# One transformer layer on one core: the residual's sum on VectorE in half rows, a new order of the input's first steps, HGRN output one step later, hints on two branches

## The chip, the cores and the metric

The kernel runs on one core of a Trainium2 chip. TensorE (PE in the rows, PEld for its weight loads) multiplies, VectorE (DVE) and ScalarE (ACT) work element by element, GpSimd (POOL) does so too, and SyncE (SP) issues the transfers from device memory. Each engine takes its instructions in order; "PEq", "SPq" and so on in a row are the queue side of an engine. The metric is the time of one execution in microseconds on the device.

## The reference, cut to what matters

256 tokens of 1024 features, one layer, float32 throughout.

```
x = layer_norm(x, ln_in_g, ln_in_b)
h = x @ w_in + b_in                      # 14 blocks of 512 columns and 8 forget gates
fox_o = fox_attention(fq, fk, fv, log_sigmoid(ff))           # 8 heads
o = hgrn2_chunkwise(silu(hq), (1 - lb) * sigmoid(-hf), hi, logf)   # 8 heads
o = rms_norm(o) * hgrn_norm_g * silu(hg)
mixed = (sigmoid(g0) * (fox_o @ w_fox) + sigmoid(g1) * (o @ w_hgrn)) @ w_mix_out + b_mix_out
x = layer_norm(ALPHA * x + mixed, ln1_g, ln1_b)
x = layer_norm(ALPHA * x + moe(x), ln2_g, ln2_b)   # 16 experts, top 2 of the top group
```

## The kernel before, in words

**The front** (to about 250 us) is everything up to the router. The weights of the mixer come as 15 "front tiles" of 2 MB through a ring of three slots (`load_front`, line 84). Each front tile is cut into 8 units of 512 columns. Every product is made in three passes of exact halves: `prep(u)` (lines 159 to 166) casts a unit to `hi` on ScalarE (line 164; three units on VectorE, line 162) and subtracts to get `lo` on VectorE or on GpSimd (line 165, chosen by `on_pool(u)`), and `mm(u)` multiplies (lines 185 to 187 for "tm" tiles, 198 to 200 for "fm" tiles). The main loop runs over steps `i = 2 .. 59`; a step is two units, 2i and 2i+1, and in it come, in this order: `pe[i]`, `prep(2i+3)`, `mm(2i)`, the evacuation of finished products, `post[i]`, `prep(2i+4)`, `mid[i]`, `mm(2i+1)`. The tables `pe`, `mid` and `post` are filled by `at(table, step, function)` and so set by hand the order on PE, ACT, DVE and POOL. SyncE's order is left to the scheduler. A ring slot is free for the next front tile when the last unit of the old one has been prepared.

**What the change touches.** `x_turn`, `x_affine`, `x_hi`, `x_lo` bring the normalised input to features on partitions as halves (lines 225 to 250); they and the first four units stand before the loop. `resid` (lines 316 to 322) turns `xraw`, the normalised input, into `ALPHA * (x * g + b) + b_mix`, for the sum ahead of the first norm at step 53 and later (`mix_add`). `small` makes the lower bounds `lbt` of the forget gates. `h_exps(j)`, `h_mul(j)`, `h_scores(j)`, `h_mask(h)`, `h_out(h)` are the HGRN heads, two heads for each j: decays, scaled queries and keys (DVE, ACT), scores (PE), masked copies `hst` (DVE, ACT), and the sums of values (PE, lines 577 to 579). `h_check` loads a flag on four engines (line 593) and branches on it (line 594): over code for extreme decays, which these inputs do not take. A second such branch (line 1484) stands near the end, over code for experts' lists that are too long.

**The experts** (from about 250 us) take their weights, 201 MB, through some eleven slots of 2 MB. A slot's next load is issued where the instructions that read the old weights stand (`load_exp`, `load_parts`: lines 864 and 891), and waits on SyncE's queue until they are done. The front's ring becomes three of these slots. The first expert's weights are loaded during the front.

Of the kernel before, what the change touches and what calls it, by code (L numbers as in the profile page):

```python
# [23 lines left out]
# the last two experts: the down projection's weights come by columns, a half and two quarters  # L24
LAST = NE - 2

# columns of the constant pack
# [8 lines left out]
# columns of the row pack  # L36
# [10 lines left out]
def trunk(ctx: ExitStack, tc: tile.TileContext, x, cst_d, rows_d, wf, we, lvl_d, out):  # L47
# [24 lines left out]
    def bank(tag, shape, name=None):  # L72
        """one bank; g: products and all that comes and goes, s: scores, o: sums kept for long"""
        return ps.tile(shape, F32, name=name or tag, tag=tag, bufs={"g": 4, "s": 2, "o": 2}[tag])

    # ---- loads, in the order of use
# [57 lines left out]
    def stats(tt, c, src, n=256):  # L134
        """pieces of a row, of equal widths"""
        V.bn_stats(sm[:, 24 * tt + 6 * c:24 * tt + 6 * c + 6], src)

    def ln_scale(tt, n):
        """(mean, 1/sqrt(var + eps))"""
        mv = mvs(tt)  # L140
        V.bn_aggr(mv, sm[:, 24 * tt:24 * tt + 6 * n])
        A.activation(mv[:, 1:2], mv[:, 1:2], AF.Sqrt, bias=eps_in[:, 0:1])
        V.reciprocal(mv[:, 1:2], mv[:, 1:2])
        return mv

    # ---- products in three passes of exact halves; a unit: 512 columns of a weight tile
# [4 lines left out]
    def on_pool(u):  # L151
        return u in (0, 1, 2) or 24 <= u < 56 and u % 2 == 1 or u >= 56 and u % 4 == 3
# [19 lines left out]
    def mm(u, tts=(0, 1)):  # L172
# [3 lines left out]
        if KIND[i] == "tm":  # L176
            for tt in tts:
                if c == 0:
                    # the very last sums in two banks, so that their ends can overlap
# [24 lines left out]
    # ---- input norm  # L204
    def halves(name):
        """exact halves of eight blocks of features, in four parts"""
# [16 lines left out]
    def x_turn(tt, j):  # L223
        """two blocks of features, a bank each pair"""
# [28 lines left out]
    def x_parts(tt, j):  # L253
# [13 lines left out]
    warm(2, 128)  # L267
    prep(0)
    prep(1)
    x_affine(0, 0)  # L270
    x_affine(0, 1)
    x_stats(1)
    x_hi(0, 0)
    x_hi(0, 1)
    x_lo(0, 0)
    mm(0, (0,))
    V.bn_aggr(mvs(1), sm[:, 24:36])
    x_lo(0, 1)
    mm(1, (0,))
    prep(2)  # L280
    A.activation(mvs(1)[:, 1:2], mvs(1)[:, 1:2], AF.Sqrt, bias=eps_in[:, 0:1])
# [33 lines left out]
    # residual with the output bias: alpha * (x * g + b) + b_mix  # L315
    gA, bA, bM = inr
    resid = [lambda: (G.tensor_scalar(bA, bA, ALPHA, 0.0, op0=OP.mult, op1=OP.add),
                      G.tensor_scalar(gA, gA, ALPHA, 0.0, op0=OP.mult, op1=OP.add)),
             lambda: G.tensor_add(bA, bA, bM)]
    for tt in range(2):  # L320
        resid.append(lambda tt=tt: G.tensor_mul(xraw[:, tt, :], xraw[:, tt, :], gA))
        resid.append(lambda tt=tt: G.tensor_add(xraw[:, tt, :], xraw[:, tt, :], bA))

    # lower bounds of the forget gates: cumsum(softmax) - its first row, over one layer
# [7 lines left out]
    def small():  # L332
        V.tensor_tensor(e0, C("lb"), C("lb"), op=OP.subtract)
        # exp(x) as sigmoid(x) / sigmoid(-x)
        A.activation(e1, e0, AF.Sigmoid, scale=-1.0)
        A.activation(e0, e0, AF.Sigmoid)
        V.reciprocal(e1, e1)
# [5 lines left out]
        V.tensor_scalar(nbhf, C("bhf"), -1.0, None, op0=OP.mult)  # L343
# [14 lines left out]
    # tensors of the mixer  # L358
# [48 lines left out]
    # ---- HGRN2  # L407
# [7 lines left out]
    def hgrn_general(oh):  # L415
        """the same scores for any decays: pairs of tokens by the highest bit in which they differ;
        every exponent is at most zero"""
# [3 lines left out]
        for j in range(4):  # L421
# [38 lines left out]
            # between chunks: from the end of the key's chunk to the start of the query's  # L460
# [43 lines left out]
    def h_exps(j):  # L504
# [7 lines left out]
        # half of the chunk's decay as the reference point: exponents of both signs, at most  # L512
        # half the decay; beyond SAFE the general path below recomputes the scores
# [6 lines left out]
        # between chunks: from the key's reference point to the query's  # L520
# [18 lines left out]
    # two heads side by side: each on its half of the tensor engine's rows  # L539
# [21 lines left out]
    def transposed(p, val, sts, j):  # L561
        """two heads' sums of values: features on partitions, the scores' keys there too"""
# [28 lines left out]

    def h_check():
        big = nc.values_load(hfl, engines=(ET.PE, ET.Activation, ET.DVE, ET.Pool), min_val=0, max_val=1)
        with tc.If(big > 0):  # L594
# [19 lines left out]
    def feat_pe(ot):  # L614
        """[tokens, 512] to features on partitions"""
# [10 lines left out]
    # ---- forgetting attention  # L626
# [6 lines left out]
    def f_proj():  # L633
        """the eight blocks of features on four groups of columns"""
# [17 lines left out]
    def f_log():  # L652
        """log forget gates, tokens on partitions"""
# [3 lines left out]
        # log_sigmoid(f) = min(f, 0) + log(sigmoid(|f|))  # L657
# [11 lines left out]
    def f_sum(j):  # L669
        """cumulative gates of the keys, on every partition: columns as the scores'"""  # L670
# [28 lines left out]
    def f_soft(h):  # L699
        """negated logits; F[t] is the same along a row and cancels under the row's maximum"""  # L700
# [39 lines left out]
    # ---- merge gates, branches, output projection  # L740
# [53 lines left out]
    # router's weights with the norm's scale, each column centred: (r - mean) @ w = r @ centred w  # L794
# [32 lines left out]
    # ---- stream of the experts' weights: in the order of use, two experts at a time  # L827
# [10 lines left out]
    def load_exp(pl, n=1):  # L838
        for _ in range(n):
# [5 lines left out]
            if nxt[0] >= len(order) - 4:  # L845
                # in pairs, a part of each by turns
# [20 lines left out]
    # slots of four parts, the first that are used, so that loads go on as early as can be. One tile lies apart:  # L867
    # half of it comes before, with the first tile's second half, the rest in that one's place
# [3 lines left out]
    def slot(pl):  # L872
        """a slot's parts"""
# [20 lines left out]
    def claim(pl):  # L894
        """the next tile's place, its parts to be loaded one by one"""
# [717 lines left out]
```

## Time and profile before

| what | us |
|---|---|
| three runs | 703.16, 705.47, 705.56 |
| their median | 705.47 |
| span of the profiled execution (first to last instruction) | 704.5 |
| PE busy in it | 661.4 (94%) |
| mean granted clock of PE | 0.974 |
| DVE, ACT, POOL busy | 210.1, 188.5, 93.1 |
| moved by transfers | 238.75 MB, mean 339 GB/s |

The profiled execution's own time is not listed apart from its span; the span lies 1.0 us under the median of the runs and inside their range. Matmuls are pipelined, so a busy PE in a row is not PE at its peak. [...]

### The profile page before, as it was taken

The page shows a single profiled execution, that of the slowest core. Times are in us where ns is not written, and L with a number is a line of the kernel's source. Part 1 is how long each engine was busy: PE and PEld are TensorE (multiplying, and loading weights), DVE is VectorE, ACT ScalarE, POOL GpSimd, SP SyncE. Part 2 cuts the span into 40 slices and gives each one's busy share as a digit, 9 for nine tenths or more (in the row PEclk, how much of TensorE's full clock was granted, in tenths as well). Part 3 has the DMA queues.
Part 4 walks back from the last instruction along what each step waited for, and adds up shares of the span by engine and source line. Part 5 has one row for each costly group of instructions (what it writes and reads, how often), then busy time and mean ns, then how long its engine had stood idle before and what let it go on. Part 6 is the DMA issues. An engine that isn't in the chain of part 4 may idle for free.

```text
span 704.5 us, 9357 instructions
## 1 busy us (share of the span) xinstructions
PE 661.4 (94%) x3707; PEld 388.1 (55%) x3707; DVE 210.1 (30%) x457; ACT 188.5 (27%) x389; POOL 93.1 (13%) x83
## 2 busy tenths in 40 slices
PE   6779998999999999999999999999999999699986
PEld 5678797899998953534534443443443433243433
DVE  5776862654468521100100100100100100100015
ACT  4536354577645421102012010010010010010211
POOL 2632344433136000000000000000000000000001
PEclk8979999999999999999999999999999999999999
DMA  8926633543978969999999999999999999999981
GB/s 330 382 105 225 270 121 123 194 178 118 360 287 300 397 206 375 425 394 429 425 407 424 421 412 421 424 412 421 420 417 419 418 420 416 418 425 410 412 331 60
DMA packets 40520, 238.75 MB, mean 339 GB/s; under 512 B 4496, under 2 KB 4624, under 8 KB 32400
## 3 DMA queue, kind: packets, MB, share of 16 engines
q1 hardware_dynamic: 40464, 238.02, 84.3%
q8 instruction: 33, 0.54, 0.3%
q14 instruction: 23, 0.19, 0.1%
HBM read 236.95 MB, written 1.05 MB: 338 GB/s over the span
## 4 chain that ended last, share of the span: by engine, by line
PE 67%; DMA 13%; DVE 2%; ACT 0%; issue 0%; DVEq 0%; SPq 0%; ACTq 0%
PE g L1276 25%; DMA w<-in_we_dram 13%; PE g L1293 13%; PE g L1248 3%; PE g L198 3%; PE g L199 3%; PE g L200 3%; PE acc L1301 3%; PE g L186 1%; PE g L187 1%; PE g L185 1%; PE g L1312 1%; PE g L1422 1%; PE g L1284 1%; PE g L1116 1%; DVE e L1465 1%
## 5 line engine op out<-in xcount | busy, mean ns | idle before, releaser
L1276 PE MATMUL g<-w,e 128*64 128x512 f32 x992 | 219.7, 595 | 2.4 <-DMA w<-in_we_dram 2.4
L1276 PEld LDWEIGHTS g<-w,e 128*64 128x64 f32 x992 | 69.0, 137 | 138.6 <-issue 125.8
L1293 PE MATMUL g<-w,f 128*64 128x512 f32 x448 | 106.5, 604 | 2.4 <-DMA w<-in_we_dram 2.4
L165 DVE TENSOR_TENSOR lo<-w,hi 128x512 fp32r<-128x512 f32 x85 | 69.1, 824 | 62.1 <-ACT hi L164 61.3
L164 ACT CAST hi<-w 128x512 fp32r<-128x512 f32 x117 | 70.4, 620 | 54.2 <-PE g L199 39.3
L198 PE MATMUL g<-xp,hi 128*128 128x256 f32 x256 | 76.3, 298 | 9.0 <-DVE hv L374 9.0
L199 PE MATMUL g<-xp,hi 128*128 128x256 f32 x256 | 74.2, 290 | 0.0
L200 PE MATMUL g<-xp,lo 128*128 128x256 f32 x256 | 74.0, 289 | 0.0
L1293 PEld LDWEIGHTS g<-w,f 128*64 128x64 f32 x448 | 39.2, 138 | 59.5 <-issue 54.5
L1523 POOL TENSOR_TENSOR e<-e,par 128x256 f32<-128x256 f32 x2 | 1.4, 726 | 459.4 <-DVE nmr L1519 459.4
L165 POOL TENSOR_TENSOR lo<-w,hi 128x512 fp32r<-128x512 f32 x35 | 47.4, 1357 | 109.6 <-ACT hi L164 109.6
L198 PEld LDWEIGHTS g<-xp,hi 128*128 128x128 f32 x256 | 50.8, 199 | 11.3 <-issue 10.4
L199 PEld LDWEIGHTS g<-xp,hi 128*128 128x128 f32 x256 | 50.9, 199 | 0.1
L200 PEld LDWEIGHTS g<-xp,lo 128*128 128x128 f32 x256 | 50.8, 199 | 0.0
L1479 DVE COPY f<-g 128x512 f32<-128x512 f32 x7 | 4.8, 692 | 115.2 <-PE g L1293 115.2
L1248 PEld LDWEIGHTS g<-e,raw 128*128 128x128 f32 x224 | 26.1, 191 | 19.8 <-DVE e L1240 10.0
L1248 PE MATMUL g<-e,raw 128*128 128x128 f32 x224 | 28.7, 281 | 8.1 <-DVE e L1240 8.1
L1259 ACT ACTIVATE e<-g,cst 128x128 f32<-128x128 f32 x28 | 10.6, 457 | 68.7 <-PE g L1248 68.7
L1463 DVE TENSOR_TENSOR e<-e,g 128x512 f32<-128x512 f32 x8 | 5.5, 688 | 73.5 <-ACT e L1462 73.5
L185 PE MATMUL g<-hi,xp 128*128 128x512 f32 x48 | 20.7, 431 | 6.5 <-PEq L594 3.4
L1471 ACT COPY f<-g 128x512 f32<-128x512 f32 x8 | 4.7, 586 | 79.9 <-PE g L1284 79.9
L1301 PE MATMUL acc<-f,e 128*128 128x512 f32 x56 | 25.9, 605 | 0.0
(318 smaller groups left out, 745.5 us busy)
## 6 DMA issues: line engine op xcount, KB each, us to landing
w<-in_we_dram SPq DMA_DIRECT2D x49, 2048.0 KB, 17.7
w<-in_we_dram SPq DMA_DIRECT2D x178, 512.0 KB, 10.4
w<-in_wf_dram SPq DMA_DIRECT2D x13, 2048.0 KB, 8.4
w<-in_wf_dram SPq DMA_DIRECT2D x8, 512.0 KB, 9.1
w<-in_we_dram SPq DMA_DIRECT2D x16, 256.0 KB, 6.0
rbc<-in_rows_dram SPq DMA_DIRECT2D x1, 1036.0 KB, 15.9
f<-in_we_dram SPq DMA_DIRECT2D x4, 256.0 KB, 7.6
out_dram<-par SPq DMA_DIRECT2D x4, 256.0 KB, 2.1
```

The lines of the kernel that those rows point to most:

```text
L164: A.copy(hi, src)
L165: (G if on_pool(u) else V).tensor_sub(lo, src, hi.bitcast(F32))
L185: PE.matmul(p, rh(c)[:, t], hi[:, a:b], start=c == 0, stop=False, skip_group_check=True)
L186: PE.matmul(p, rh(c)[:, t], lo[:, a:b], start=False, stop=False, skip_group_check=True)
L198: PE.matmul(p, hi[:, w], rh(k), start=k == 0, stop=False)
L199: PE.matmul(p, hi[:, w], rl(k), start=False, stop=False)
L200: PE.matmul(p, lo[:, w], rh(k), start=False, stop=k == nk - 1)
L1248: PE.matmul(p[:, i, :], raw[:, tt, k * 128:(k + 1) * 128], oneh2[:, tt, :], start=tt == 0, stop=tt == 1)
L1259: A.activation(t[:, i, :], p[:, i, :], AF.Identity, bias=C("b1")[:, 4 + i:5 + i], scale=C("g1")[:, 4 + i:5 + i])
L1276: PE.matmul(h[64 * nh:64 * nh + 64, :], xg[kh][:, k, 64 * (e % 2):64 * (e % 2) + 64], wcol(e, m + kh, k, nh), start=kh + k == 0, stop=kh = ...
L1293: PE.matmul(py[nh][64 * a:64 * a + 64, :], hT[a][:, c0:c0 + 64], wt[:, nh * 512:nh * 512 + 512], start=f == 0, stop=f == 7)
L1301: PE.matmul(acc[tt][nh], GT[:, tt, :], y[nh], start=start, stop=False, skip_group_check=True)
```

## The change

It does six things. (1) The residual's sum moves from seven GpSimd instructions on 1024 columns at steps 4 to 9 to ten VectorE instructions on 512 columns, one at each of the steps 5 to 14, with ALPHA folded in. (2) Units 0 and 1 get their `lo` on VectorE, no more on GpSimd. (3) The first four steps of the input (`x_affine` to `x_lo` for its first two pairs of blocks) stand ahead of `prep(0)`, and six warming products stand in the place of two. (4) `small` is cut in two: its first part stands at step 2, the rest (`small1`) at step 3. (5) `h_out` stands one step later. (6) Each of the two branches gets a hint, "LikelyTaken", on four engines.

```diff
-        return u in (0, 1, 2) or 24 <= u < 56 and u % 2 == 1 or u >= 56 and u % 4 == 3
+        return u == 2 or 24 <= u < 56 and u % 2 == 1 or u >= 56 and u % 4 == 3
...
-    warm(2, 128)
+    warm(6, 128)
+    x_affine(0, 0)
+    x_affine(0, 1)
+    x_hi(0, 0)
+    x_lo(0, 0)
+    x_hi(0, 1)
+    x_lo(0, 1)
     prep(0)
     prep(1)
-    x_affine(0, 0)
-    x_affine(0, 1)
+    mm(0, (0,))
     x_stats(1)
-    x_hi(0, 0)
-    x_hi(0, 1)
-    x_lo(0, 0)
-    mm(0, (0,))
     V.bn_aggr(mvs(1), sm[:, 24:36])
-    x_lo(0, 1)
     mm(1, (0,))
+    A.activation(mvs(1)[:, 1:2], mvs(1)[:, 1:2], AF.Sqrt, bias=eps_in[:, 0:1])
     prep(2)
-    A.activation(mvs(1)[:, 1:2], mvs(1)[:, 1:2], AF.Sqrt, bias=eps_in[:, 0:1])
...
-    resid = [lambda: (G.tensor_scalar(bA, bA, ALPHA, 0.0, op0=OP.mult, op1=OP.add),
-                      G.tensor_scalar(gA, gA, ALPHA, 0.0, op0=OP.mult, op1=OP.add)),
-             lambda: G.tensor_add(bA, bA, bM)]
+    resid = []
+    for h in range(2):
+        resid.append(lambda c=slice(512 * h, 512 * h + 512): V.scalar_tensor_tensor(
+            bA[:, c], bA[:, c], ALPHA, bM[:, c], op0=OP.mult, op1=OP.add))
     for tt in range(2):
-        resid.append(lambda tt=tt: G.tensor_mul(xraw[:, tt, :], xraw[:, tt, :], gA))
-        resid.append(lambda tt=tt: G.tensor_add(xraw[:, tt, :], xraw[:, tt, :], bA))
+        for h in range(2):
+            c = slice(512 * h, 512 * h + 512)
+            resid.append(lambda tt=tt, c=c: V.scalar_tensor_tensor(
+                xraw[:, tt, c], xraw[:, tt, c], ALPHA, gA[:, c], op0=OP.mult, op1=OP.mult))
+            resid.append(lambda tt=tt, c=c: V.tensor_add(xraw[:, tt, c], xraw[:, tt, c], bA[:, c]))
...
+    def h_hint():
+        tc.mark_branch_hint_location("hgrn", "LikelyTaken", engines=ENG4)
...
-        with tc.If(big > 0):
+        with tc.If(big > 0, label="hgrn"):
...
-    at(post, 3, small)
+    at(post, 2, small)
+    at(post, 3, small1)
...
-        at(post, 4 + n, r)
+        at(post, 5 + n, r)
...
-            at(pe, 17 + 2 * j, h_out, h)
+            at(pe, 18 + 2 * j, h_out, h)
...
+    at(post, 23, h_hint)
...
+        if e == LAST:
+            tc.mark_branch_hint_location("slots", "LikelyTaken", engines=ENG4)
```

In the built program both hints stand at the very start of each of the four engines, not where they are marked; the one for the second branch ("slots") stands ahead of the one for the first ("hgrn"). On SyncE, three of the first expert's loads and one of 2 MB move ahead of the load of front tile 6, which they stood behind or around.

On VectorE, steps 2 to 5 of the loop: `lbt` are the bounds that `small` makes, `lo` the lower halves of units 7 to 11, `hv` the first front tile's finished products, taken out of PSUM. Before:

```order
L165 TENSOR_TENSOR lo<-w,hi 128x512 x4
L333 TENSOR_TENSOR lbt<-cst 128x4
L337 RECIPROCAL lbt<-lbt 128x4
L338 TENSOR_TENSOR lbt<-lbt 128x4
L339 RECIPROCAL lbt<-lbt 128x4
L340 TENSOR_TENSOR lbt<-lbt 128x4
L341 TENSOR_TENSOR lbt<-lbt 128x4
L342 TENSOR_SCALAR lbt<-lbt 128x4
L343 TENSOR_SCALAR lbt<-cst 128x4
L165 TENSOR_TENSOR lo<-w,hi 128x512 x2
L374 TENSOR_TENSOR hv<-g,rbc 128x512 x2
L165 TENSOR_TENSOR lo<-w,hi 128x512 x2
```

and in the changed kernel:

```order
L166 TENSOR_TENSOR lo<-w,hi 128x512 x2
L338 TENSOR_TENSOR lbt<-cst 128x4
L342 TENSOR_SCALAR lbt<-cst 128x4
L166 TENSOR_TENSOR lo<-w,hi 128x512 x2
L345 RECIPROCAL lbt<-lbt 128x4
L346 TENSOR_TENSOR lbt<-lbt 128x4
L347 RECIPROCAL lbt<-lbt 128x4
L348 TENSOR_TENSOR lbt<-lbt 128x4
L349 TENSOR_TENSOR lbt<-lbt 128x4
L350 TENSOR_SCALAR lbt<-lbt 128x4
L166 TENSOR_TENSOR lo<-w,hi 128x512 x2
L381 TENSOR_TENSOR hv<-g,rbc 128x512 x2
```

The same instructions stand ahead of `hv`, two of the small ones now ahead of two `lo`.

On VectorE, steps 12 and 13: `ff` and `lfr` are the forget gates of the attention, which wait for a logarithm on ScalarE, `B` to `Dd` the first decays of the HGRN heads. Before:

```order
L384 SCALAR_TENSOR_TENSOR hqt<-g,cst,hqt 128x256
L664 TENSOR_SCALAR ff<-ff 128x16
L665 TENSOR_TENSOR ff<-ff 128x16
L666 CAST lfr<-ff 128x16
L667 TENSOR_TENSOR lfr<-ff,lfr 128x16
L162 CAST hi<-w 128x512
L165 TENSOR_TENSOR lo<-w,hi 128x512
L510 SCALAR_TENSOR_TENSOR B<-rst,lf 128x256
L515 TENSOR_SCALAR hrg<-B 128x4
```

and in the changed kernel:

```order
L391 SCALAR_TENSOR_TENSOR hqt<-g,cst,hqt 128x256
L327 TENSOR_TENSOR raw<-raw,in_inb 128x512
L674 TENSOR_SCALAR ff<-ff 128x16
L675 TENSOR_TENSOR ff<-ff 128x16
L676 CAST lfr<-ff 128x16
L677 TENSOR_TENSOR lfr<-ff,lfr 128x16
L163 CAST hi<-w 128x512
L166 TENSOR_TENSOR lo<-w,hi 128x512
L325 SCALAR_TENSOR_TENSOR raw<-raw,in_ing 128x512
L517 SCALAR_TENSOR_TENSOR B<-rst,lf 128x256
L522 TENSOR_SCALAR hrg<-B 128x4
```

One instruction of the residual is new ahead of `ff`, and one ahead of `B`; a third stands ahead of the products of step 14.

On PE, HGRN output of heads 0 and 1 (`o<-hv,hst`) stood alone between two units of products, step 17:

```order
L200 MATMUL g<-xp,lo 128x256
L577 MATMUL o<-hv,hst_116 128x64
L578 MATMUL o<-hv,hst_116 128x64
L579 MATMUL o<-hv,hst_116 128x64
L577 MATMUL o<-hv,hst_117 128x64
L578 MATMUL o<-hv,hst_117 128x64
L579 MATMUL o<-hv,hst_117 128x64
L198 MATMUL g<-xp,hi 128x256
```

and in the changed kernel, step 18:

```order
L584 MATMUL o<-hv,hst_116 128x64
L585 MATMUL o<-hv,hst_116 128x64
L586 MATMUL o<-hv,hst_116 128x64
L584 MATMUL o<-hv,hst_117 128x64
L585 MATMUL o<-hv,hst_117 128x64
L586 MATMUL o<-hv,hst_117 128x64
L555 MATMUL s<-qp,kp 128x128 x2
L557 MATMUL s<-qx,kp 64x64 x2
L555 MATMUL s<-qp,kp 128x128 x2
L557 MATMUL s<-qx,kp 64x64 x2
L560 MATMUL s<-qx,kx 128x128 x2
```

It stands right ahead of the next pair's scores, two units of products later.

## Rows read from the trace of the kernel before

**Rows 1.** The page: GB/s moved, in 40 equal slices of 17.6 us.

```profile
GB/s 330 382 105 225 270 121 123 194 178 118 360 287 300 397 206 375 425 394 429 425 407 424 421 412 421 424 412 421 420 417 419 418 420 416 418 425 410 412 331 60
```

**Rows 2.** Stretches: busy us and instructions of each engine, clock, DMA share, GB/s.

```profile
core 0: us, PE busy (x) PEld busy (x) DVE busy (x) ACT busy (x) POOL busy (x), PEclk, DMA share, GB/s
...
31.40:40.40 9.00, 0.01 (x2) 0.03 (x1) 8.93 (x8) 0.90 (x3) 8.84 (x5) 0.76 0.32 136
40.40:46.00 5.60, 5.59 (x27) 5.60 (x27) 3.91 (x6) 0.93 (x2) 1.47 (x1) 0.50 0.00 0
46.00:63.50 17.50, 17.50 (x147) 17.50 (x146) 11.50 (x25) 10.60 (x22) 1.29 (x1) 0.99 0.53 189
82.20:87.20 5.00, 5.00 (x29) 5.00 (x30) 4.90 (x15) 1.70 (x5) 1.58 (x1) 0.66 1.03 428
121.30:124.70 3.40, 3.40 (x10) 2.62 (x9) 1.29 (x2) 1.21 (x3) 1.28 (x1) 0.51 0.00 0
...
260.00:680.00 420.00, 404.75 (x1918) 164.86 (x1914) 41.89 (x70) 46.78 (x98) 0.00 (x0) 1.00 1.01 414
```

**Rows 3.** SyncE's waits, 225 to 262 us: total, times, longest.

```profile
SPq L891 <- PE g L1422: 13.7, 6, 9.3
```

**Rows 4.** The chain that ended last, 575 us to the end: start, us, what.

```profile
589.55 10.18 DMA w<-in_we_dram
...
676.35 4.47 DMA w<-in_we_dram
...
680.95 3.52 PE g L1312 x16
```

**Rows 5.** PE's waits, 0 to 250 us: total, times, longest.

```profile
PE g L198 <- DVE hv L374: 9.0, 1, 9.0
PE g L185 <- PEq L594: 3.4, 1, 3.4
PE o L577 <- DVE hst L558: 1.5, 1, 1.5
```

**Rows 6.** Timeline of POOL, 24 to 66 us: last of the residual's seven.

```profile
39.19 2.69 POOL L322 TENSOR_TENSOR raw<-raw,in_inb 128x1024 f32<-128x1024 f32 x1
```

**Rows 7.** Timeline of DVE, 24 to 66 us.

```profile
29.48 2.12 DVE L340 TENSOR_TENSOR lbt<-lbt 128x4 f32<-128x4 f32 x1
31.63 2.26 DVE L341 TENSOR_TENSOR lbt<-lbt 128x4 f32<-128x4 f32 x1
33.93 0.17 DVE L342 TENSOR_SCALAR lbt<-lbt 128x4 f32<-128x4 f32 x1
...
36.23 3.43 DVE L165 TENSOR_TENSOR lo<-w,hi 128x512 fp32r<-128x512 f32 x2
39.58 1.27 DVE L374 TENSOR_TENSOR hv<-g,rbc 128x512 f32<-128x512 f32 x2
```

**Rows 8.** Groups of DVE by line and form, 46 to 64 us.

```profile
L165 DVE TENSOR_TENSOR lo<-w,hi 128x512 fp32r<-128x512 f32 x11 | 7.6, 692 | 6.2 <-ACT hi L164 6.0
```

**Rows 9.** Timeline near the end.

```profile
699.63 0.73 DVE L1534 SCALAR_TENSOR_TENSOR par<-par,sm,g 128x512 f32<-128x512 f32 x1
```

**Rows 10.** Line 594, the first branch on PE: least, middle and most ns, start.

```profile
L594 PEldq COMPARE_BRANCH  x1: 5280/5280/5280, 114.8 to 114.8; - x1
```

**Rows 11.** Timeline, the first 50 us, all engines.

```profile
9.01 1.14 ACT L164 CAST hi<-w 128x512 fp32r<-128x512 f32 x2 [3.49 <-DMA w<-in_wf_dram]
9.71 3.92 POOL L165 TENSOR_TENSOR lo<-w,hi 128x512 fp32r<-128x512 f32 x3 [8.56 <-ACT hi L164]
...
11.20 0.50 PE L185 MATMUL g<-hi,xp 128*128 128x512 f32 x1 [3.08 <-ACT xp L245]
```

**Rows 12.** Timeline of DVE, 64 to 135 us: steps 12 to 14.

```profile
67.33 0.17 DVE L665 TENSOR_TENSOR ff<-ff 128x16 f32<-128x16 f32 x1 [1.76 <-ACT ff L663]
...
73.08 1.52 DVE L532 TENSOR_TENSOR kp<-kp,hk 128x256 f32<-128x256 f32 x1
```

**Rows 13.** Timeline of POOL, the same stretch.

```profile
73.00 2.75 POOL L165 TENSOR_TENSOR lo<-w,hi 128x512 fp32r<-128x512 f32 x2 [3.59 <-ACT hi L164]
```

More of the change, by code (lines that the diff above doesn't have):

```diff
@@ L23 @@
 SAFE = 40.0
+ENG4 = (ET.PE, ET.Activation, ET.DVE, ET.Pool)
 LAST = NE - 2
@@ L336, in small, with small1 @@
         A.activation(e0, e0, AF.Sigmoid)
+        V.tensor_scalar(nbhf, C("bhf"), -1.0, None, op0=OP.mult)
+    def small1():
         V.reciprocal(e1, e1)
@@ L342, in small @@
         V.tensor_scalar(omlb, lb, -1.0, 1.0, op0=OP.mult, op1=OP.add)
-        V.tensor_scalar(nbhf, C("bhf"), -1.0, None, op0=OP.mult)
     def small2():
@@ L1483, in trunk @@
     tm = wt.pop()
-    with tc.If(over > 0):
+    with tc.If(over > 0, label="slots"):
         more_slots()
```

## The prediction

> **What bounds the kernel now.** I read the end first, by the chain of work that ended last. From 589.55 us on it is almost only transfers of experts' weights; the last ends at 680.82, and the last expert's products start 0.13 us behind it [rows 4]. The table of stretches shows why: between 260 and 680 us the DMA engines are full (share 1.01, 414 GB/s), while PE, busy 404.75 of 420 us, has a little room [rows 2]. So the second part of the kernel is a stream of 420 x 414 = 174 MB, and what a kernel can gain there is to start it earlier.
>
> Then I asked what holds its start, by SyncE's waits: between 225 and 262 us loads wait 13.7 us for the first expert's products on PE, up to 9.3 us at once, because the slots are still in use [rows 3]. The row of GB/s says the same from the other side: slices 3, 6, 7 and 10 move 105 to 123 GB/s, and only from slice 16 on is it 375 or more, until the last two [rows 1]. Before about 260 us the transfers have room and follow PE. My reading is that one microsecond taken out of PE's front moves the whole stream, and the end, by one.
>
> So what does PE lose in the front? Its list of waits names four things the change touches: 9.0 us for `hv` from DVE, 3.4 us at the branch of line 594, 1.5 us for `hst` [rows 5], and 3.08 us for the first `xp` [rows 11]. [...]
>
> **(1) The residual leaves GpSimd.** While PE waits 9.0 us, DVE is busy 8.93 of it and POOL 8.84 [rows 2]: PE waits for DVE, and DVE is slow. An operation on 128x4 with two inputs takes 2.12 and 2.26 us, the next one with one input 0.17; two `lo` take 3.43 [rows 7], where a `lo` on 128x512 otherwise takes 0.692 [rows 8]. Beside them POOL runs the residual, whose last instruction ends at 41.88 [rows 6]. Without it I price the two small ones at 0.17 each (4.04 saved), the one that fills 34.10 to 36.23 likewise (2.0 saved), the two `lo` at 1.38 (2.05 saved): `hv` would come 8.1 us sooner by these alone. The small ones ahead of them start sooner too, so the saving lies between 8.1 and 9.0; I take 8.6. The 5.6 us at half clock behind it [rows 2] give 2.8 at most, nothing if small waits keep the clock low; since DVE's 3.91 us of work there leave it little slack, I take 2.6. **-11.2 us** (-8.1 to -11.8). The order shows no new instruction ahead of `hv`, so nothing replaces this wait at once; `hv` itself stays the next thing that is late, by some tenths.
>
> [...]
>
> **(1, other half) Ten instructions come to DVE.** The nearest row is 0.73 us for a SCALAR_TENSOR_TENSOR on 128x512 [rows 9], the `lo` 0.692: ten cost about 7 us. Seven stand at steps 5 to 11, a stretch of about 17.5 us in which DVE is busy 11.50 [rows 2]; 11.5 + 5.1 = 16.6 still fits, with PE as cover; were it gone, they would cost up to 5. Step 12's lands ahead of `ff`, which waits 1.76 us for ScalarE anyway [rows 12]. Those of 13 and 14 stand where DVE is already slowed, `kp` taking 1.52 us [rows 12] as a POOL `lo` pair of 2.75 us begins [rows 13], and what waits behind them on DVE are the operands of the first HGRN scores on PE. I charge nearly all of two: **+1.3 us** (0 to +5).
>
> **(2, 3, 4) The first steps.** PE's first product starts at 11.20 after a wait of 3.08 [rows 11]. In the new order ScalarE makes `xp` before it casts the weights; these landed at 9.01, and one cast takes 0.57 (half of 1.14), so the first product can't start before 9.58: 1.6 us at most. The two `lo` on DVE take 1.4 us in place of the three of 3.92 on POOL [rows 11]. If the shorter gap also spared PE a stretch of low clock like the others, as much as 2.8 more could come. Against it, DVE and ScalarE bear the same work up to `hv` and one part of `small` a step sooner. **-1.0 us** (0 to -4.4).
>
> **(5) HGRN output a step later.** PE waits 1.5 us for `hst` [rows 5], and the next 5.0 us run at 0.66, a loss of 5.0 x 0.34 = 1.7 [rows 2]. A step lasts about 17.5 / 7 = 2.5 us, more than the 1.5 by which `hst` is late, so the wait should vanish. **-3.0 us** (-1.5 to -3.2); the rest is for the PSUM that is held a step longer.
>
> **(6) Hints.** PE's branch instruction stands 5.28 us [rows 10]; the next product comes 3.4 us late [rows 5], and 3.4 us at 0.51 follow, 1.7 lost [rows 2]: 5.1 if the hint takes it all, 0 if it does nothing. No row here shows a hinted branch. I take it that the hint works, less 0.6 for what on ScalarE and DVE hid behind this wait: **-4.5 us**. The second branch is worth nothing, since the transfer at 680.82 ends as late as before.
>
> **SyncE's order.** Four loads pass front tile 6. DMA is idle from 40.4 to 46.0 and at 0.53 up to 63.5 [rows 2], which covers them; I price this at 0. If the three are half a megabyte each, the four are 3.5 MB, 8.5 us at 414 GB/s, which is what PE would wait without that cover.
>
> **Sum.** -11.2 + 1.3 - 1.0 - 3.0 - 4.5 = -18.4, from the span of 704.5: 686.1. The median of the runs is 1.0 above that span, so **687.1 us**.
>
> **The rivals.**
>
> *The hints do nothing.* Then -13.9: 691.6 us. For it: both hints stand at the program's start, 115 us ahead of the branch, so whatever they prepare must last; against it, the wait is the branch's own [rows 10] and something like it must be what a hint is for. [...]
>
> *DVE becomes the bound at steps 12 to 14.* If each residual instruction there meets a POOL `lo` and stands like the small one did (2.26 us [rows 7]) or longer, and delays the scores, with low clock behind: three times 2.3 and 1 to 2 us of clock, in place of the 1.3: 6 to 7 us worse, 693 to 698. Front tile 6 arriving late would give about the same. For it: [rows 13]; against: POOL runs one or two `lo` per step, and DVE has waits to give.
>
> *The gain stays in the front.* If the stream could not start earlier, because something other than PE's use of slots holds it, the end stays at about 705 us. Against it: the waits of [rows 3] name PE.
>
> [...]
>
> **How the numbers follow.** I give the forecast 0.55, the idle hints 0.33, the blocked DVE 0.06, the gain lost in the front 0.03, the costly hint 0.03. The hint's chance is little more than even because no row bears on it. The forecast's own range is 684 to 690. The range for everything runs from 683, where the first steps and the clock give back nearly all they can, to 695, which takes in the idle hints with 3 us of further loss and the better half of the blocked DVE. A change of 0.5% (3.5 us) is about what a measurement of this kernel tells from none. Faster by more: 0.55 + 0.33 + 0.06 = 0.94; the same 0.03; slower 0.03.
>
> **What the changed kernel's profile would show.** (1) PE's 9.0 us wait for `hv` is below 1 us, clock 0.9 or more behind it, and the small `lbt` operations take 0.2 us each. PE's waits at steps 12 to 14 stay below 2 us in sum. (2 to 4) First product near 9.8. (5) No wait of `o` for `hst`. (6) The branch instruction on PE lasts well under 1 us and the clock holds; if it lasts 5 us again, the first rival has it. In the table of stretches the full stream begins some 18 us sooner, and the last transfer ends near 662. The prediction is wrong if PE's waits go and the last transfer doesn't move, if a wait of several microseconds for DVE or for front tile 6 appears, or if the hint is idle.

## The result and the profile after

Four runs of the changed kernel took 685.88 to 689.79 us, median 687.62; four of before on the same chip 703.16 to 707.04, median 705.51. The ratio is 0.9763 with a 95% interval of 0.973 to 0.9796: faster, by 17.9 us in the medians. The forecast was 687.1. The profiled execution has a span of 688.0.

The four waits of [rows 5] and [rows 11] are gone or small. This is the list of PE's waits of the changed kernel from 0 to 250 us (total, times, longest), the rows that belong to the steps of the prediction:

```profile
PE g L229 <- DVE raw L220: 1.7, 1, 1.7
...
PE g L187 <- DVE lo L166: 1.4, 4, 0.7
...
PE g L593 <- DVE hrg L589: 0.6, 1, 0.6
PE s L555 <- DVE kp L539: 0.3, 1, 0.3
...
PE g L186 <- ACT xp L246: 0.2, 1, 0.2
```

No wait for `hv`, `hst` or the branch is left in it. Two are new: 1.7 us for `raw`, at 13.1 us, in the first steps, and 0.6 us for `hrg`, the least of the HGRN decays that the first branch's flag is made from, at 87.5 us. The table of stretches of the changed kernel (busy us and instructions of each engine, clock, DMA share, GB/s) shows the clock (PEclk, a share of full speed) at 1.00 behind `hv`, the HGRN output and the first branch, where [rows 2] has 0.50 to 0.66, and the same full stream, 415 GB/s, in the second part. Behind the second branch, in the last row, it is 0.50:

```profile
core 0: us, PE busy (x) PEld busy (x) DVE busy (x) ACT busy (x) POOL busy (x), PEclk, DMA share, GB/s
11.20:19.00 7.80, 5.64 (x27) 4.01 (x27) 6.50 (x15) 3.77 (x9) 2.05 (x2) 1.00 1.02 427
30.00:40.00 10.00, 10.00 (x84) 10.00 (x85) 9.06 (x22) 6.32 (x16) 0.00 (x0) 1.00 0.88 347
66.00:72.00 6.00, 6.00 (x54) 6.00 (x52) 4.79 (x16) 3.42 (x9) 1.32 (x2) 1.00 0.45 191
72.00:80.00 8.00, 8.00 (x73) 7.44 (x72) 6.72 (x19) 3.42 (x9) 3.11 (x3) 1.00 0.16 33
100.00:106.00 6.00, 5.85 (x31) 4.66 (x30) 1.29 (x2) 4.57 (x8) 2.37 (x2) 1.00 0.60 253
260.00:662.00 402.00, 386.80 (x1824) 157.84 (x1820) 39.14 (x64) 44.21 (x94) 0.00 (x0) 1.00 1.01 415
663.30:667.00 3.70, 3.66 (x17) 1.99 (x17) 0.00 (x0) 0.00 (x0) 0.00 (x0) 0.50 0.90 333
```

DVE's timeline, against [rows 7]: the small operations take 0.17 us, a pair of `lo` 1.28, and `hv` starts at 28.80 in place of 39.58. The residual's half rows take 0.68, and up to 1.12 where a GpSimd `lo` runs beside them.

```profile
27.32 0.17 DVE L349 TENSOR_TENSOR lbt<-lbt 128x4 f32<-128x4 f32 x1
...
27.60 1.28 DVE L166 TENSOR_TENSOR lo<-w,hi 128x512 fp32r<-128x512 f32 x2
28.80 1.28 DVE L381 TENSOR_TENSOR hv<-g,rbc 128x512 f32<-128x512 f32 x2
...
48.99 1.12 DVE L325 SCALAR_TENSOR_TENSOR raw<-raw,in_ing 128x512 f32<-128x512 f32 x1
```

And the two branches on PE (least, middle and most ns, first and last start), the first against [rows 10]:

```profile
L604 PEldq COMPARE_BRANCH  x1: 401/401/401, 100.4 to 100.4; - x1
```

```profile
L1498 PEldq COMPARE_BRANCH  x1: 4651/4651/4651, 658.4 to 658.4; - x1
```

The first is short now, the second is not. Where it stands PE waits. In the timeline of PE near the end the bracket is the idle time before an instruction and what ended it:

```profile
657.63 1.93 PE L1324 MATMUL g<-w,f 128*64 128x512 f32 x6 [0.21 <-DMA w<-in_we_dram]
663.34 3.68 PE L1324 MATMUL g<-w,f 128*64 128x256 f32 x16 [3.79 <-PEq L1498]
666.95 2.97 PE L1331 MATMUL acc<-f,e 128*128 128x512 f32 x4
```

In [rows 4] the same products, at 680.95, are put down to a transfer; here they are put down to the branch. The trace of before speaks for the branch there too. The transfer that [rows 4] names was issued at 676.35 and took 6.0 us to land, so it landed when those products had already started. PE's second branch of before stood for 4.19 us, to 680.6, and it is what the weight loads of these products waited for. The rows of the transfer, of the branch and of the weight loads:

```profile
L853 SPq DMA_DIRECT2D w<-in_we_dram x1: 328/328/328, 676.4 to 676.4; - x1
...
DMA to landing us min/median/max: 6.0/6.0/6.0
```

```profile
L1484 PEldq COMPARE_BRANCH  x1: 4187/4187/4187, 676.5 to 676.5; - x1
```

```profile
680.92 1.02 PEld L1312 LDWEIGHTS g<-w,f 128*64 128x64 f32 x8 [3.26 <-PEq L1484]
```

The best reading of where time went comes from matching the same product on PE in both traces (start in us), behind each stretch of low clock once the clock is up again in both:

| where PE is | before | after | difference |
|---|---|---|---|
| last products before `hv` is read | 27.60 | 26.05 | -1.55 |
| behind `hv` and its low clock | 46.30 | 33.20 | -13.10 |
| step 14, ahead of the first HGRN output | 78.34 | 66.45 | -11.89 |
| the next pair's scores, behind that output in both | 88.17 | 72.85 | -15.32 |
| last but a few ahead of the first branch | 115.31 | 100.71 | -14.60 |
| behind the branch and its low clock | 126.81 | 107.35 | -19.46 |
| the router | 247.20 | 227.53 | -19.67 |
| an expert's products in the full stream | 400.05 | 380.25 | -19.80 |
| last expert, last products ahead of the second branch's wait | 677.10 | 658.11 | -18.99 |
| last expert, behind it | 680.95 | 663.34 | -17.61 |
| end of the span | 704.5 | 688.0 | -16.5 |

So the front gained 19.7 us and the stream moved by 19.8, as the reading of [rows 3] says. Then 3.3 us were given back at the end: 0.8 ahead of the second branch, where PE waits for weights that are not yet there (the 0.21 us at 657.63 is one such wait), 1.4 at the branch (a wait of 3.79 us in place of the 2.41 us before 680.95), and 1.1 behind it, where the clock is low for longer (0.50 from 663.3 to 667.0 and still 0.67 from 667.0 to 670.0; in before 0.54 from 680.9 to 684.4, then 0.98 to 690.0). The total hit the forecast with two errors in it that cancel: a little more in the front, a loss at the end. The spans differ by 16.5 us and the medians by 17.9; the profiled execution of the changed kernel was the slowest of its four.

### The profile page after: what moved, and what is told of

Its sections match the earlier page's. It is cut to its first block, busy times and chain, and to the rows that moved or that the text cites. A ratio compares the mean times of both kernels' runs of the same rounds, so it can differ in the third digit from the quotient of the medians.

```text
span 688.0 us, 9379 instructions
## 1 busy us (share of the span) xinstructions
PE 657.4 (96%) x3715; PEld 380.5 (55%) x3715; DVE 205.6 (30%) x469; ACT 187.7 (27%) x389; POOL 75.9 (11%) x74
## 5 line engine op out<-in xcount | busy, mean ns | idle before, releaser
L1288 PE MATMUL g<-w,e 128*64 128x512 f32 x992 | 222.3, 598 | 3.5 <-DMA w<-in_we_dram 3.5
L166 DVE TENSOR_TENSOR lo<-w,hi 128x512 fp32r<-128x512 f32 x87 | 67.7, 789 | 51.0 <-ACT hi L165 50.1
L199 PE MATMUL g<-xp,hi 128*128 128x256 f32 x256 | 74.3, 290 | 0.0
L201 PE MATMUL g<-xp,lo 128*128 128x256 f32 x256 | 72.5, 283 | 0.2 <-DVE lo L166 0.2
L200 PE MATMUL g<-xp,hi 128*128 128x256 f32 x256 | 72.4, 283 | 0.0
L166 POOL TENSOR_TENSOR lo<-w,hi 128x512 fp32r<-128x512 f32 x33 | 45.2, 1371 | 110.7 <-ACT hi L165 110.7
L199 PEld LDWEIGHTS g<-xp,hi 128*128 128x128 f32 x256 | 48.9, 191 | 2.6 <-issue 1.4
L201 PEld LDWEIGHTS g<-xp,lo 128*128 128x128 f32 x256 | 49.0, 191 | 0.4 <-DVE lo L166 0.4
L200 PEld LDWEIGHTS g<-xp,hi 128*128 128x128 f32 x256 | 49.0, 191 | 0.0
L1475 DVE TENSOR_TENSOR e<-e,g 128x512 f32<-128x512 f32 x8 | 5.5, 687 | 73.5 <-ACT e L1474 73.5
L1462 DVE TENSOR_TENSOR e<-e,g 128x512 f32<-128x512 f32 x8 | 5.5, 688 | 64.1 <-PE g L1288 64.1
```

Of the source, the lines that this page charges most:

```text
L166: (G if on_pool(u) else V).tensor_sub(lo, src, hi.bitcast(F32))
L199: PE.matmul(p, hi[:, w], rh(k), start=k == 0, stop=False)
L200: PE.matmul(p, hi[:, w], rl(k), start=False, stop=False)
L201: PE.matmul(p, lo[:, w], rh(k), start=False, stop=k == nk - 1)
L1288: PE.matmul(h[64 * nh:64 * nh + 64, :], xg[kh][:, k, 64 * (e % 2):64 * (e % 2) + 64], wcol(e, m + kh, k, nh), start=kh + k == 0, stop=kh = ...
```

## The experiments

The medians below are of 4 to 6 runs each (two for the memsets). Those of before, on the same chips, were 703.56 to 706.48. Medians of kernels that lie within 2 us of each other are not told apart by them; there the traces decide.

**Which branch has a hint.** Four kernels from the changed one. `no_hints` leaves out both calls, `slots_only` the first branch's:

```diff
-    at(post, 23, h_hint)
```

> The changed kernel without both hints. Theory A (the hint on the first branch made it short): PE's branch instruction at line 604 takes 5 us again instead of 0.40, the front gives back the 4.5 us seen across it, time 692 (687.6 + 4.5); the second branch stays at 4 to 5 us on PE, as with the hint. Rival B (the branch got short because the code around it moved, not by the hint): 0.4 us and 687.6 without hints too.

> The changed kernel with the second branch's hint alone, at the program's start. Theory A1 (an engine keeps one hint, the one it executed last, and with both that was the first branch's): the first branch takes 5 us on PE, the second falls from 4.65 to under 1 us, and the 3.8 us that PE waits there in the changed kernel go but for the transfers' own lateness of about 1.5: time 692.1 - 2 = 690. Theory A2 (a hint does not last for 650 us): both branches take 4 to 5 us, 692. Rival A3 (hints only help a branch that they come shortly before, and the second had one all the time): as A2.

The other two keep the first hint and take the second from a register. The built program then sets that hint where its register is loaded, inside the last pair of experts, and no more at the program's start:

```diff
         if e == LAST:
-            tc.mark_branch_hint_location("slots", "LikelyTaken", engines=ENG4)
+            again = nc.values_load(hfl, engines=ENG4, min_val=0, max_val=1)
+            tc.mark_branch_hint_location("slots", again, engines=ENG4)     # late_hint0; late_hint1: 1 - again
```

> The changed kernel with the second branch's hint taken from a register (value 1), which puts it behind the first branch, some 13 us of PE's work ahead of the second; it adds a load of a flag on four engines. Theory A1 (one hint at a time, the last one counts): both branches are under 1 us on PE, PE's wait of 3.8 us there falls to the 1.0 to 2 us by which the weights are late, time 687.6 - 2 = 685.5. If hints hold more than one or the second branch cannot be helped: 4.65 us at the second branch as before, 687.6 or some tenths more for the load.

> The same with the register's value 0. If the value says whether the branch will be taken (0: no), the second branch stays at 4 to 5 us on PE: 687.6. If the value does not matter: as with value 1, 685.5. If only one of the two values shortens the branch, that one carries the hint.

| kernel | median us | ratio to before, interval | first branch on PE, ns | second, ns |
|---|---|---|---|---|
| changed kernel | 687.62 | 0.9763 (0.973 to 0.9796) | 401 | 4651 |
| `no_hints` | 693.5 | 0.9836 (0.978 to 0.9892) | 5737 | 3927 |
| `slots_only` | 690.69 | 0.9785 (0.9729 to 0.9841) | 5499 | 380 |
| `late_hint1` | 687.74 | 0.9747 (0.9689 to 0.9805) | 409 | 4398 |
| `late_hint0` | 683.62 | 0.9696 (0.964 to 0.9752) | 402 | 439 |

The branch rows of `slots_only`, one for each branch, and of `late_hint0`:

```profile
L604 PEldq COMPARE_BRANCH  x1: 5499/5499/5499, 100.4 to 100.4; - x1
```

```profile
L1497 PEldq COMPARE_BRANCH  x1: 380/380/380, 665.5 to 665.5; - x1
```

```profile
L1499 PEldq COMPARE_BRANCH  x1: 439/439/439, 657.8 to 657.8; - x1
```

Without hints the first branch is long again, so rival B (moved code) is out. Behind it PE is 5.7 us later than in the changed kernel (113.01 against 107.35), 0.3 of it from ahead of the branch, so a little more than the 4.9 of the table above. `slots_only` settles the second point: a hint given at the program's start still serves a branch at 665.5 us (380 ns), so A2 and A3 are out, and the changed kernel's second hint was not too early. It was lost: with both at the start only the one that the engine executed last had an effect (401 ns, against 4651 for the other's branch). That one is also the hint of the branch that comes first, and no kernel here swaps the two, so which of these counts is not shown. `late_hint0` has both branches short and is 4.0 us under the changed kernel (4.1 under `late_hint1`, which ran on the same chip), more than the 2 expected: its last products start 3.9 us sooner (659.47 against 663.34), and PE then runs at a higher clock (on average 0.95 from 657.0 to 681.6, against 0.85 from 663.3 to 688.0; the first sixteen products take 1.95 us in place of 3.68). The 1 to 2 us by which the weights were expected to be late did not show: PE waits 0.30 us there. In `late_hint1` the weight loads of these products wait 4.3 us for the branch, in `late_hint0`, with only the register's value changed, 1.1. The row to hold against 666.95 above, from PE's timeline of `late_hint0`, is the four sums of 128x512, 1.98 us in place of 2.97:

```profile
659.47 1.95 PE L1324 MATMUL g<-w,f 128*64 128x256 f32 x16 [0.30 <-PEq L1499]
661.34 1.98 PE L1331 MATMUL acc<-f,e 128*128 128x512 f32 x4
```

The register's value counts: with 0 the branch takes 439 ns, with 1 4398. These inputs make the condition 0.

**The residual, alone and undone.** `resid_only` is before with nothing but the residual's ten half rows on VectorE; `resid_back` is the changed kernel with the seven GpSimd instructions.

```diff
# resid_back
-        at(post, 5 + n, r)        # ten, V.scalar_tensor_tensor / V.tensor_add
+        at(post, 4 + n, r)        # seven, G.tensor_scalar / G.tensor_mul / G.tensor_add
```

> The kernel before with the residual's sum alone moved to VectorE as ten half rows, steps 5 to 14; nothing else changed. Theory C (GpSimd's residual instructions blocked VectorE's two-input ones ahead of hv): PE's 9.0 us wait for hv falls below 1.5 us, the small lbt operations take 0.2 us, the clock behind stays at 0.9 or more, time 705.5 - 11.2 + 1.3 = 695.6. Rival D (the wait needs the other edits too: lbt's split or the new start): hv still late by 4 us or more, 699 to 705.

> The changed kernel with the residual back on GpSimd, seven instructions at steps 4 to 9. Theory C: PE waits 8 to 10 us for hv again, half clock behind it, 687.6 + 11 - 1.2 = 697.5. Rival D: the earlier start and the split of lbt keep hv in time, 688 to 692.

`resid_only` took 693.87 us (0.9849, 0.9804 to 0.9894), `resid_back` 697.93 (0.9897, 0.9851 to 0.9944). In `resid_only` PE has no wait for `hv`, and what it gains between the products at 27.60 and 46.30 of before is 11.6 us (-2.27 to -13.91; the first 2.3 are a start that happened to be earlier). In `resid_back` the loss behind `hv` is 10.3 us (from 0.75 to 11.09 later than in the changed kernel). Rival D is out both ways. PE's wait in `resid_back`:

```profile
PE g L199 <- DVE hv L377: 8.6, 1, 8.6
```

and the two engines beside each other, DVE, then GpSimd:

```profile
28.12 0.17 DVE L341 RECIPROCAL lbt<-lbt 128x4 f32<-128x4 f32 x1
28.32 2.15 DVE L342 TENSOR_TENSOR lbt<-lbt 128x4 f32<-128x4 f32 x1
...
30.71 2.05 DVE L344 TENSOR_TENSOR lbt<-lbt 128x4 f32<-128x4 f32 x1
32.80 0.16 DVE L345 TENSOR_TENSOR lbt<-lbt 128x4 f32<-128x4 f32 x1
32.99 2.20 DVE L346 TENSOR_SCALAR lbt<-lbt 128x4 f32<-128x4 f32 x1
```

```profile
27.61 2.83 POOL L320 TENSOR_TENSOR in_inb<-in_inb,in_bmix 128x1024 f32<-128x1024 f32 x1
30.40 2.34 POOL L322 TENSOR_TENSOR raw<-raw,in_ing 128x1024 f32<-128x1024 f32 x1
32.82 2.34 POOL L323 TENSOR_TENSOR raw<-raw,in_inb 128x1024 f32<-128x1024 f32 x1
```

The reader sees that the held instruction on DVE ends just when GpSimd's ends (30.47 and 30.44; 32.76 and 32.74; 35.19 and 35.16), and that a small one slips through between two of them, at 32.80. The one that slips through has two inputs, and the last one held, a TENSOR_SCALAR, has one. The RECIPROCAL at 28.12, one input too, is not held: it takes 0.17 us while GpSimd's at 27.61 runs on to 30.44.

**Reading or only being busy.** Two kernels add work to GpSimd in the changed kernel, at steps 4 to 9, into a tile that nothing reads:

```diff
+    for n in range(6):
+        for _ in range(8):
+            at(post, 4 + n, lambda: G.memset(scr, 0.0))                                # dummy_write
+            at(post, 4 + n, lambda: G.tensor_add(scr, gA[:, 0:160], gA[:, 0:160]))     # dummy_read
```

> The changed kernel with 48 GpSimd memsets of 128x160 into a scratch tile that nothing reads, eight at each of the steps 4 to 9: GpSimd is busy some 12 us there but reads nothing from SBUF. Theory P (a two-input VectorE instruction is held only by a GpSimd instruction that reads SBUF): the small lbt operations stay at 0.2 us, hv in time, 687.6. Rival Q (any GpSimd activity at that place holds VectorE, or PE's wait came from GpSimd's own order): small operations slowed to 0.3 us and more, hv late by 2 us or more, 690 or more.

> The same with 48 GpSimd additions of 128x160 that read the gain's tile and write the scratch tile. Theory P: every two-input VectorE instruction beside them waits for at most the one GpSimd instruction that is running, here about 0.4 us in place of 2.4; the small lbt operations take 0.3 to 0.6 us, lo 0.9 to 1.2, hv comes 2 to 4 us later than in the changed kernel, PE waits 1 to 3 us, 689 to 692. Rival Q: as the memsets. Rival R (the hold lasts for the whole burst, not for one instruction): hv late by 8 us or more, 697.

With the memsets (48 in 13.96 us from 24.73 on), a pair of `lo` takes 1.29 us, two-input `lbt` operations 0.16, `hv` starts at 29.15: 0.35 later than in the changed kernel, not 10, and that much late is already the `lo` at 23.39, ahead of the memsets. Theory P holds for two-input operations, rival Q does not. The one-input TENSOR_SCALAR on `lbt` took 0.30 us in place of 0.17. The two runs, 691.1 us, don't tell this kernel from the changed one; in its trace PE is 0.6 us late by the router and 2.6 at 400 us, and why was not settled.

With the additions `lbt` operations take up to 0.31 us (0.28 with two inputs), a pair of `lo` 1.53, and `hv` starts at 30.04, 1.24 us later, 0.41 of it from ahead of the additions; PE waits 0.5 us for it. No `lbt` operation is longer by more than 0.14 us, a small part of one addition (0.78, the middle value below) and not the whole burst of 36.64, so rival R is out; theory P had the kind right and expected more of it (2 to 4 us at `hv`, against 0.8). But the time is 699.03 us (0.9932, 0.9904 to 0.996), not 689 to 692. The reason is on the other engine: GpSimd's 48 additions took 36.64 us in all. One took 0.45 us at least, as those at 24.8 and 55.4 us with VectorE idle beside them, and 0.78 as the middle value of the 48 (least, middle and most ns in the row below). GpSimd's own first `lo` came behind them. GpSimd's additions, its timeline and PE's wait:

```profile
L940 POOL TENSOR_TENSOR scr<-in_ing x48: 451/780/982, 24.8 to 61.0; 128x160 f32<-128x160 f32 x48
```

```profile
24.82 36.64 POOL L940 TENSOR_TENSOR scr<-in_ing 128x160 f32<-128x160 f32 x48
61.42 2.49 POOL L166 TENSOR_TENSOR lo<-w,hi 128x512 fp32r<-128x512 f32 x2
```

```profile
PE g L187 <- POOL lo L166: 8.7, 1, 8.7
```

**HGRN output at its old place.** Only the step is put back:

```diff
-            at(pe, 18 + 2 * j, h_out, h)
+            at(pe, 17 + 2 * j, h_out, h)
```

> The changed kernel with HGRN output back at steps 17, 19, 21 and 23. Theory B: PE waits 1 to 2 us for hst at the first of them, then runs some 5 us at a clock of about 0.66, 3 us in all: 690.6. Rival B0: in the changed kernel the masked copies are early enough, no wait: 687.6.

Median 689.69 us (0.9785, 0.9745 to 0.9825), not told apart from the changed kernel. The trace shows theory B: the wait of [rows 5] is back, 1.5 us, and the clock behind it is 0.79 on average.

```profile
PE o L584 <- DVE hst L565: 1.5, 1, 1.5
```

```profile
72.00:80.00 8.00, 8.00 (x59) 7.37 (x59) 6.16 (x18) 2.60 (x9) 2.85 (x2) 0.79 0.14 29
```

PE is 3.6 us late at the next pair's scores, where both kernels have made the first output, and 2.9 us late at the first branch (0.2 of each from the start). The 0.7 between them is what the later output gives back; the wait for `hrg` (0.65 us), which `hout_early` does not have, stands in that stretch.

**The first steps in their old order**, on the changed kernel and on the fastest version (`best_d`, next):

```diff
-    warm(6, 128)
-    x_affine(0, 0)
...
+    warm(2, 128)
     prep(0)
     prep(1)
+    x_affine(0, 0)
...
-        return u == 2 or 24 <= u < 56 and u % 2 == 1 or u >= 56 and u % 4 == 3
+        return u in (0, 1, 2) or 24 <= u < 56 and u % 2 == 1 or u >= 56 and u % 4 == 3
```

> The changed kernel with the first steps in the order of before: weights' casts ahead of xp on ScalarE, two warming products, lo of units 0 and 1 on GpSimd (small stays cut in two). Theory S (the prediction's term): first product 1 to 2 us later, low clock from about 13 to 19 us, PE 1 us later where hv is read, 688.6. Rival S0: what PE wins there it waits for again before step 4, since the weights' landing and ScalarE set the pace; the product that reads hv starts at the same time within 0.5 us, 687.6. Rival S3: the low clock costs its full 2.9 us, 690 to 691.

> The fastest version so far (late hint of value 0, residual packed into steps 5 to 11; 681.74) with the first steps in the order of before. In the changed kernel that edit put PE 1.9 us back at the router but only 0.2 us at the last expert's products, behind the 4.65 us of the second branch. Theory E (that branch swallowed the difference, since PE sat in it either way): here, where the branch is short, the 1.5 to 2 us of the front reach the end, 683.5. Rival F (the transfers' own landing at the end swallows it): 681.7, and the last products start at the same time within 0.5 us of 657.4.

`startup_old` took 689.65 us (0.9774, 0.9741 to 0.9806), `best_startup_old` 683.09 against 681.74: each 1.3 to 2.0 slower, neither told apart by its runs. The two traces disagree. In the first, PE waits 2.6 us for the first `xp`, its clock is 0.50 from 11.2 to 15.0 and 0.69 to 19.0, and it is 1.5 us late where `hv` is read and 1.9 at the router. In the second, where the first product came at 10.03 and not 11.16, it waits 1.41, the clock stays at 1.00, and PE is 0.6 us ahead of `best_d` from 17 us to 400 us, and 0.6 behind at the last expert. The stretches of `startup_old` and of `best_startup_old`:

```profile
11.20:15.00 3.80, 3.68 (x8) 2.04 (x9) 3.76 (x7) 1.63 (x4) 2.38 (x2) 0.50 1.07 445
15.00:19.00 4.00, 4.00 (x18) 3.34 (x17) 2.80 (x8) 2.08 (x6) 0.73 (x1) 0.69 0.99 423
```

```profile
11.20:15.00 3.80, 2.73 (x13) 2.04 (x14) 3.76 (x9) 1.65 (x5) 1.27 (x1) 1.00 1.06 441
15.00:19.00 4.00, 4.00 (x21) 3.10 (x20) 2.94 (x8) 1.77 (x5) 0.74 (x1) 1.00 0.98 414
```

Theory E (the second branch swallowed the difference) is left open: in the second kernel the front had nothing to swallow. The other traces say the same of the order. The product that stands at 27.60 in before starts at 25.33 (`resid_only`), 25.50, 27.52 and 27.60 in the four kernels with the old order, the two late ones with the clock at 0.69 and 0.50 from 15 to 19 us, the two early ones at 1.00; in the ten with the new order it starts between 26.05 and 27.08. So the old order stood 1.5 us behind the changed kernel there in two traces and 0.6 to 0.7 ahead of it in two.

**No residual at steps 12 to 14.** `best_d` is `late_hint0` with

```diff
-        at(post, 5 + n, r)
+    for n, r in zip((5, 6, 7, 8, 9, 9, 10, 10, 11, 11), resid):
+        at(post, n, r)
```

> The kernel with the late hint of value 0, and the residual's ten half rows packed into steps 5 to 11 (two at each of 9, 10 and 11) so that none stands at steps 12 to 14. Theory C1 (those three cost PE about 1.2 us, since kp and lo behind them come late): PE's three small waits between steps 12 and 14 go, 683.6 - 1.2 = 682.4. Rival C2 (steps 9 to 11 have no room for three more: VectorE is busy 8.3 of 10 us there): new waits of PE for lo of the same size, 683.6 or up to 2 us more.

It took 681.74 us (0.9683, 0.9653 to 0.9714), the fastest kernel here, by the ratios 3.2% under before and 0.8% under the changed one; against `late_hint0` the runs don't tell it apart. In its trace no new wait of PE stands at steps 9 to 11, the 0.3 us for `kp` is gone, and PE's lead over `late_hint0` grows from 0.9 us, its size from 26 to 60 us, to 2.1 at the first scores: 1.2 us, as C1 expected. One of the three waits, 0.7 us for `lo`, stays; before has it too (0.70 us at 70.01).

## Why the prediction was right, and where it was not

**What bounds the kernel** held: 19.7 us out of the front moved the stream by 19.8. The rival that the gain stays in the front is out. **SyncE's order**, priced at 0, held too: no wait for a front tile's transfer stands among PE's waits.

**(1) The residual off GpSimd**: forecast -11.2, measured -11.55 in the table, 11.6 in `resid_only`, 10.3 in `resid_back`. That the residual's instructions held VectorE's is shown by these two kernels and the pairs of ends in `resid_back`; the two dummies show that it was not GpSimd's being busy alone: two-input operations on 128x4 took 0.16 us beside the memsets, which read nothing, and up to 0.28 beside the additions, which read. The rival that this bites back on VectorE at steps 12 to 14 did not come: the half rows took 0.68 to 1.12 us, not 2.3.

One reading in this step was wrong, without harm to its sum. The prediction set 2.26 us with two inputs against 0.17 with one. The 0.17 at 33.93 [rows 7] fell into the gap between two GpSimd instructions; the next one, with one input as well, took 2.31 us and ended with GpSimd's (36.32 and 36.29), VectorE first, then GpSimd:

```profile
34.01 2.31 DVE L343 TENSOR_SCALAR lbt<-cst 128x4 f32<-128x4 f32 x1
```

```profile
31.53 2.34 POOL L321 TENSOR_TENSOR raw<-raw,in_ing 128x1024 f32<-128x1024 f32 x1
33.95 2.34 POOL L322 TENSOR_TENSOR raw<-raw,in_inb 128x1024 f32<-128x1024 f32 x1
```

So the number of inputs alone does not tell what is held: TENSOR_SCALAR was (2.31 here, 2.20 in `resid_back`), RECIPROCAL was not (0.17 and 0.18 in `resid_back`, at 28.12 and 30.50). What sets the two apart is not shown.

**(1, other half)**: forecast +1.3, measured +1.2 from step 5 to step 14 (-13.10 to -11.89). `best_d`, with none of the ten at steps 12 to 14, gains 1.2 there, and `resid_back`, with none of them at all, 1.2 (from 11.09 late to 9.87).

**(2 to 4)**: forecast -1.0, measured -1.55 in this pair of traces, which the other traces don't bear out as the change's doing: against the changed kernel the old order was 1.5 us late in two of them and 0.6 to 0.7 us ahead in two. The first product did come 2.0 us sooner (9.23, below the 9.58 taken as the least, since the weights were there by 8.56 in this execution), but PE then waits 1.7 us for `raw`, a wait that the prediction did not have. The low clock, for which it allowed up to 2.8 us, stands from 15 to 19 us in the late traces (0.69 and 0.50) and not in the early ones (1.00). That -1.0 is near -1.55 is luck; the sign of this term is not settled.

**(5)**: forecast -3.0, measured -2.7 between step 14 and the branch (3.4 by the next scores, 0.7 given back), and 2.7 when it is undone in `hout_early`. The wait for `hrg` in that 0.7 was not foreseen.

**(6)**: forecast -4.5 for the first branch, measured -4.9 in the table, 5.4 in `no_hints` and 5.05 in `slots_only`. The rival that hints do nothing is out, and the costly hint, given 0.03, did not come: the kernel is faster by 17.9 us. On PE the branches without an effective hint took 3.9 to 5.7 us, those with one 0.38 to 0.44; what the long ones wait for is not shown here.

**The step that failed** is the sentence "The second branch is worth nothing, since the transfer at 680.82 ends as late as before." It took the last wait for a transfer's. The runs show the branch in its place: the transfer that [rows 4] names landed after the products had started, their weight loads waited for the branch, and in `late_hint0`, where the branch is short, PE waits 0.30 us there and the kernel takes 4.0 us less. The price of 0 did no harm to the sum, since the hint on this branch had no effect in the changed kernel. But the branch, with late weights ahead of it and a clock of 0.50 behind it, gave back 3.3 us of the gain. How much before would gain from a short second branch alone was not run. That the total came out within 0.5 us owes something to this loss: the terms of the front alone sum to -18.4 in the forecast and -19.7 in the trace.

## What to carry to other kernels

An engine that is busy all through a stall, as DVE was for 8.93 of 9.00 us here, may be held, not working: compare the same small operation beside the other engine's instructions and away from them, and look at what ends when it ends. When a wait's row names a transfer, look when that transfer landed and what else ended there; here it was a branch. Match products where the clock is up again in both traces, or part of the gain is left out. Two hints at the program's start did the work of one here: give the second after the first branch is past, and read each branch's duration, not the source, to see which one works.

## What the runs showed of the hardware that was not expected

- Of two hints at the program's start, the one executed last, for the branch that comes first, had an effect (401 ns, and 4651 for the other branch); a single one served the branch at 665.5 us (380 ns in place of 3927 to 4651).
- A hint from a register works with value 0 where the branch's condition is 0 (439 ns) and not with value 1 (4398 ns).
- One-input TENSOR_SCALARs on 128x4 were held by GpSimd as two-input operations were (2.31 and 2.20 us, against 2.05 to 2.26), and RECIPROCALs were not (0.17 and 0.18).
- GpSimd was slower beside VectorE, too: its additions of 128x160 took 0.45 us alone and 0.78 as the middle value of 48, most of them beside VectorE's work, and cost the kernel more through GpSimd's own late `lo` (8.7 us) than through VectorE (0.5 us of PE's wait for `hv`).
- In two kernels with the same first steps the low clock came in one and not in the other: behind a wait of 2.6 us for the first `xp` it was 0.50 (`startup_old`), behind 1.41 us it stayed at 1.00 (`best_startup_old`); and yet behind the 1.5 us wait for `hst` in `hout_early` it was 0.79. What decides this was not tested.
